# Down projection of a Strassen-type feed-forward block: product 2 in the other four PSUM banks, product 6 summed on product 1

## The chip, the cores and the metric

The kernel runs on one core of one Trainium2 chip. The metric is the device time of one execution in microseconds (us), lower is better. Each time comes from an execution on the chip; the profile is one more execution, recorded by the hardware profiler.

## The reference

The kernel computes one layer of a diffusion backbone: x is 1024 tokens by 1024 channels, all in fp32. The part that matters here is its end, with w_gate and w_up of 1024 x 2816 and w_down of 2816 x 1024:

```
def swiglu(h, w_gate, w_up, w_down):
    return (jax.nn.silu(h @ w_gate) * (h @ w_up)) @ w_down
...
x = x + g1 * mix
h2 = modulate(rmsnorm(x, norm2_g[layer]), sh2, sc2)
x = x + g2 * swiglu(h2, w_ffn_gate[layer], w_ffn_up[layer], w_ffn_down[layer])
return x
```

## The kernel before

Everything ahead of the last product, attention, projections, gate and up, is left as it is by the change. The last stage is the **down projection**, act @ w_down, and the residual x2 + g2 * (...) behind it.

The down projection is one level of the Strassen-Winograd scheme: both operands are cut into 2 x 2 blocks, and seven products of half size take the place of eight. The kernel calls them by the numbers 1, 2, 6, 7, 5, 4, 3 and runs them in this order. The seven left factors were summed before, in the feed-forward stage, and lie in DRAM (s_d). The right factors are made on the way from rows of w_down, kept in SBUF (wr, rows, lower), by `weights(n, g)`: for product 6 that is three DVE subtractions a step, of which the second writes a page t with two buffers.

A product has 11 steps g (256 rows of the inner dimension, as two halves), and each step has four output tiles i of 128 x 512. `step(n, g)` loads one page ar of the left factor by SP into the tag st (three buffers in all), makes it into a high and a low part (page a: ACT casts, DVE subtracts), and does the same with the right factor (page wd: ACT casts, POOL subtracts). Pages a and wd come from a pool yp of eight buffers, so four steps are in flight. `go` then issues three matmuls for each i: high x high, high x low, low x high. That is 12 matmuls a step, 132 a product, 924 in all.

`multiply(n, ps, first, done)` runs the 11 steps of a product on four PSUM banks ps, and calls done(i) behind the last step of tile i. `first` says whether the banks are begun anew or summed on. `banks()` takes four of the eight banks; the third call gets those of the first, the fourth those of the second. So before the change X and Z are the same four banks, and Y and W are the other four.

The outputs are put together so, with P1 to P7 for the products: u2 = P1 + P6; u3 = u2 + P7; the quarters of the output are P1 + P2 (emit(0,0)), u3 + P5 (emit(1,1)), u2 + Z, where P4 was summed on P7 (emit(1,0)), and u2 + W, where P3 was summed on P5 (written out by p3). P2 was summed on X, the banks that held P1, after ACT had copied P1 to u2; P6 went to Y and DVE added it to u2. `emit` multiplies a tile by the gate g2b, adds the residual x2t, and stores it.

The order in which each engine issues its instructions in this stage is not written by hand: a planner of the framework places them by its own forecast of when each is ready, with earlier program lines preferred, and buffers are given out by it too.

Of the kernel before, what the change touches and what calls it, by code (L numbers as in the profile page):

```python
# [13 lines left out]
ALU = mybir.AluOpType  # L14
# [74 lines left out]
def hybrid_block_kernel(  # L89
# [55 lines left out]
    PE, DVE, ACT, SP = Ordered(nc.tensor), Ordered(nc.vector), Ordered(nc.scalar), Ordered(nc.sync)  # L145
# [36 lines left out]
    def page(name, dt=F32, cols=512, tag="st"):  # L182
        return stg.tile([P, cols], dt, tag=tag, name=name)
# [74 lines left out]
    with ExitStack() as sa:  # L258
# [262 lines left out]
        for ji, (job, c0) in enumerate(jobs):  # L521
# [23 lines left out]
            for t in range(NT if job == "q" else NT + NTC):  # L545
# [29 lines left out]
                elif half:  # L575
                    st = jp.tile([P, 256], F32, tag="st", name="stc")
                    ACT.copy(st, ps[:, 256:])
                    SP.dma_start(gkc_d[(t - NT) * P:(t - NT + 1) * P, :], st)
                else:
# [10 lines left out]
                    st = jp.tile([P, 8, 64], F32, tag="st", name="str")  # L590
# [644 lines left out]
    with ExitStack() as so:  # L1235
# [62 lines left out]
        for t in range(NT - 1):  # L1298
# [3 lines left out]
            if t in E1:  # L1302
                i = len(early1)
# [70 lines left out]
    def banks3():  # L1374
        return (fps.tile([P, 512], F32, tag=n, name="f" + n) for n in "YZW")

    ops0, X, u2 = first[0]
    Y, Z, W = banks3()
# [143 lines left out]
    with ExitStack() as sf:  # L1522
# [30 lines left out]
        def step(n, g):  # L1553
            if n == 1 and g < NEARLY:
                weights(n, g)
                return early[g]
            ar = page("ar")
            r0 = (NG * (n - 1) + g) * P
            SP.dma_start(ar, s_d[r0:r0 + P, :])
            return down_pages(ar, weights(n, g), POOL)  # L1560

        def go(ps, g, a, w, i, first, last):
            s = slice(i * P, (i + 1) * P)
            st, en = first and g == 0, last and g == NG - 1
            PE.matmul(ps[i], a[:, 0, s], w[:, 0], start=st, stop=False, skip_group_check=True)
            PE.matmul(ps[i], a[:, 0, s], w[:, 1], start=False, stop=False, skip_group_check=True)
            PE.matmul(ps[i], a[:, 1, s], w[:, 0], start=False, stop=en, skip_group_check=True)

        def banks():
            return [dps.tile([P, 512], F32, tag="d", name="psdn") for _ in range(4)]  # L1570

        def multiply(n, ps, first, done, ntail=1, mid=None):
            for g in range(NG - ntail):
                if mid and g == MID:
                    mid()
                aw = step(n, g)
                for i in range(4):
                    go(ps, g, *aw, i, first, True)
            aws = [(g, *step(n, g)) for g in range(NG - ntail, NG)]
            for i in range(4):  # L1580
                for aw in aws:
                    go(ps, *aw, i, first, True)
                done(i)

        u2, u3, resid = [], [], {}
        def at(hf, c, i):
            return slice(hf * 512 + i * P, hf * 512 + (i + 1) * P), slice(c * 512, (c + 1) * 512)

        def load_x2(hf, c):
            for i in range(4):  # L1590
                t = fp.tile([P, 512], F32, tag="x2", name="x2t", bufs=NX2)
                SP.dma_start(t, x2_d[at(hf, c, i)])
                resid[hf, c, i] = t

        def emit(hf, c, i, v):
            ot = page("ot", tag="sb")
            DVE.tensor_tensor(ot, v, g2b[:, c * 512:(c + 1) * 512], op=ALU.mult)
            x2t = resid[hf, c, i]
            DVE.tensor_tensor(x2t, x2t, ot, op=ALU.add)
            SP.dma_start(out[at(hf, c, i)], x2t)  # L1600

        def p1(i):
            u2.append(fp.tile([P, 512], F32, name=f"u2{i}"))
            ACT.copy(u2[i], X[i])

        def p6(i):
            DVE.tensor_tensor(u2[i], u2[i], Y[i], op=ALU.add)

        def p7(i):
            u3.append(fp.tile([P, 512], F32, name=f"u3{i}"))  # L1610
# [17 lines left out]
        X = banks()  # L1628
# [1 line left out]
        g2b = fp.tile([P, D], F32, name="g2b")  # L1630
        SP.dma_start(g2b, mod_d[3:4, :].broadcast_to([P, D]))
        load_x2(0, 0)
        multiply(2, X, False, lambda i: emit(0, 0, i, X[i]))
        Y = banks()
        multiply(6, Y, True, p6)
        Z = banks()
        multiply(7, Z, True, p7)
        load_x2(1, 1)
# [91 lines left out]
```

## Time and profile before

| | us |
|---|---|
| runs before: median (lowest, highest) of 3 | 1598.3 (1594.61, 1601.04) |
| the profiled execution, its own time | 1597.48 |
| its span, from first to last instruction | 1595.7 |
| down projection, first to last matmul's start | 1374.9 to 1590.9 |

The profile names engines PE (TensorE matmuls), PEld (its weight loads), DVE, ACT, POOL and SP, which issues the DMAs. A row gives what an engine did, output first; an idle time in brackets is what the engine waited just before, with the instruction that ended the wait. Matmuls overlap, so the start-to-start spacing of a run of matmuls says more than the duration of one. Where the trace names tiles it leaves buffer numbers out: psdn is any of the eight banks X, Y, Z, W; u is u2 or u3.

### The profile page before, as it was taken

The page shows a single profiled execution, that of the slowest core. Times are in us where ns is not written, and L with a number is a line of the kernel's source. Part 1 is how long each engine was busy: PE and PEld are TensorE (multiplying, and loading weights), DVE is VectorE, ACT ScalarE, POOL GpSimd, SP SyncE. Part 2 cuts the span into 40 slices and gives each one's busy share as a digit, 9 for nine tenths or more (in the row PEclk, how much of TensorE's full clock was granted, in tenths as well). Part 3 has the DMA queues.
Part 4 walks back from the last instruction along what each step waited for, and adds up shares of the span by engine and source line. Part 5 has one row for each costly group of instructions (what it writes and reads, how often), then busy time and mean ns, then how long its engine had stood idle before and what let it go on. Part 6 is the DMA issues. An engine that isn't in the chain of part 4 may idle for free.

```text
span 1595.7 us, 21599 instructions
## 1 busy us (share of the span) xinstructions
PE 1531.8 (96%) x7884; PEld 1252.6 (79%) x7884; DVE 1018.4 (64%) x1598; ACT 636.1 (40%) x1221; POOL 518.1 (32%) x340
## 2 busy tenths in 40 slices
PE   6999999999999999999999999799999999999998
PEld 3678888878778887778878887688887888877886
DVE  4755469038877755553684678866666665878356
ACT  3433255158767752133212334233333333344432
POOL 3323000022211211210221422555555555256454
PEclk9999999999999999999999999999999999999999
DMA  9456666354333236416652333433333334774342
GB/s 339 128 186 215 230 220 228 107 154 125 103 114 108 87 94 218 157 58 216 225 171 67 125 120 102 150 117 100 99 100 99 99 102 129 266 255 146 99 145 99
DMA packets 171667, 235.49 MB, mean 148 GB/s; under 512 B 15580, under 2 KB 105628, under 8 KB 171560
## 3 DMA queue, kind: packets, MB, share of 16 engines
q1 hardware_dynamic: 171560, 234.11, 45.5%
q8 instruction: 62, 1.02, 0.3%
q14 instruction: 45, 0.37, 0.1%
HBM read 167.83 MB, written 66.24 MB: 147 GB/s over the span
## 4 chain that ended last, share of the span: by engine, by line
PE 76%; DVE 11%; issue 4%; DMA 4%; ACT 3%; POOL 2%; SPq 0%; DVEq 0%; ACTq 0%; POOLq 0%
PE psj L137 15%; PE psdn L137 10%; PE psd L137 9%; PE fZ L137 7%; PE fW L137 7%; PE fX L137 6%; PE pso L137 5%; PE psb L137 4%; PE fY L137 4%; PE pv L137 2%; PE pt L137 1%; ACT pb L137 1%; DVE phl L137 1%; DVE S L137 1%; DVE oT L137 1%
## 5 line engine op out<-in xcount | busy, mean ns | idle before, releaser
L137 PE MATMUL psdn<-wd,a 128*128 128x512 f32 x924 | 211.9, 390 | 4.4 <-ACT u L137 1.8
L137 PEld LDWEIGHTS psdn<-wd,a 128*128 128x128 f32 x924 | 172.7, 188 | 43.5 <-DVE a L137 3.7
L211 POOL TENSOR_TENSOR w_P<-sc,w_P 128x512 fp32r<-128x512 f32 x80 | 119.4, 1495 | 128.8 <-ACT w_P L137 125.5
L137 PE MATMUL fZ<-T,w_P 128*128 128x512 f32 x528 | 129.1, 394 | 10.3 <-DVE u L137 10.3
L211 POOL TENSOR_TENSOR w_lo<-raw,w_hi 128x1024 fp32r<-128x1024 f32 x24 | 57.6, 2400 | 235.6 <-ACT w_hi L137 218.1
L137 PE MATMUL psd<-hh,w_hi 128*128 128x512 f32 x320 | 133.4, 417 | 0.0
L137 PE MATMUL psd<-hh,w_lo 128*128 128x512 f32 x320 | 128.5, 402 | 0.0
L137 PE MATMUL psd<-hl,w_hi 128*128 128x512 f32 x320 | 127.7, 399 | 0.0
L137 PE MATMUL psj<-w_hi,hh 128*128 128x512 f32 x320 | 125.4, 393 | 0.8 <-ACT hh L137 0.8
L137 PEld LDWEIGHTS fZ<-T,w_P 128*128 128x128 f32 x528 | 100.6, 191 | 32.3 <-issue 8.9
L137 PE MATMUL psj<-w_lo,hh 128*128 128x512 f32 x320 | 125.3, 392 | 0.6 <-POOL w_lo L211 0.6
L137 PE MATMUL psj<-w_hi,hl 128*128 128x512 f32 x320 | 124.7, 393 | 0.5 <-DVE r L137 0.4
L211 POOL TENSOR_TENSOR w_P<-raw,w_P 128x512 fp32r<-128x512 f32 x56 | 87.7, 1566 | 78.0 <-ACT w_P L137 68.6
L137 ACT CAST w_P<-sc 128x512 fp32r<-128x512 f32 x88 | 54.0, 621 | 130.1 <-PE fZ L137 66.3
L137 PE MATMUL fX<-B,w_P 128*128 128x512 f32 x432 | 103.8, 389 | 0.0
L137 DVE TENSOR_TENSOR a<-ar,a 128x512 fp32r<-128x512 f32 x77 | 64.9, 855 | 58.6 <-ACT a L137 58.5
L249 POOL TENSOR_TENSOR r<-r,nhalf 128x8 f32<-128x8 f32 (+1 forms) x40 | 51.3, 1286 | 150.2 <-DVE r L137 150.2
L137 PEld LDWEIGHTS fX<-B,w_P 128*128 128x128 f32 x432 | 81.1, 188 | 16.8
L137 ACT CAST a<-ar 128x512 fp32r<-128x512 f32 x77 | 47.9, 623 | 113.9 <-PE psdn L137 64.4
L137 ACT CAST w_hi<-raw 128x1024 fp32r<-128x1024 f32 x56 | 58.1, 1049 | 53.2 <-DMA raw<-in_w_in_dram 20.3
L137 DVE SCALAR_TENSOR_TENSOR t1f<-t1f,u 128x512 f32<-128x512 f32 x66 | 61.7, 935 | 20.1 <-ACT t1f L137 19.0
L137 PEld LDWEIGHTS psj<-w_hi,hl 128*128 128x128 f32 x320 | 60.3, 189 | 14.9 <-DVE hl L137 2.4
(267 smaller groups left out, 3474.2 us busy)
## 6 DMA issues: line engine op xcount, KB each, us to landing
wm<-in_w_mod_dram SPq DMA_DIRECT2D x48, 512.0 KB
raw<-in_w_in_dram SPq DMA_DIRECT2D x40, 512.0 KB
ar<-s_d SPq DMA_DIRECT2D x77, 256.0 KB
raw<-in_w_gate_dram SPq DMA_DIRECT2D x22, 512.0 KB
raw<-in_w_up_dram SPq DMA_DIRECT2D x22, 512.0 KB
s_d<-t1f SPq DMA_DIRECT2D x44, 256.0 KB
s_d<-sa SPq DMA_DIRECT2D x33, 256.0 KB
xt<-in_x_dram SPq DMA_DIRECT2D x16, 512.0 KB
```

What stands on the lines that cost most here:

```text
L137: r = op(*args, **kw)
L211: return (lo_eng or DVE).tensor_tensor(lo, src, hi.bitcast(F32), op=ALU.subtract)
L249: POOL.tensor_tensor(r, r, nhalf[:, 0:w], op=ALU.pow)
```

## The change

Product 2 no longer sums on X but begins anew in Y, and p2 adds it to u2 (which still holds P1) in a new page v, from which emit goes on. Product 6 sums on X, which still holds P1, so X then holds P1 + P6, and ACT copies it to u2. So the four DVE additions of p6 become four ACT copies, and four DVE additions of p2 are new. The copies of P1 by p1 stay. Z still takes X's banks and W those of Y.

```
+        def p2(i):
+
+            v = page("v", tag="st")
+            DVE.tensor_tensor(v, u2[i], Y[i], op=ALU.add)
+            emit(0, 0, i, v)
+
         def p6(i):
-            DVE.tensor_tensor(u2[i], u2[i], Y[i], op=ALU.add)
+            ACT.copy(u2[i], X[i])
...
         load_x2(0, 0)
-        multiply(2, X, False, lambda i: emit(0, 0, i, X[i]))
         Y = banks()
-        multiply(6, Y, True, p6)
+        multiply(2, Y, True, p2)
+        multiply(6, X, False, p6)
         Z = banks()
         multiply(7, Z, True, p7)
```

## Rows read from the trace of the kernel before

**Rows 1.** The page's engine table: busy time, share of the span, instructions.

```profile
PE 1531.8 (96%) x7884; PEld 1252.6 (79%) x7884; DVE 1018.4 (64%) x1598; ACT 636.1 (40%) x1221; POOL 518.1 (32%) x340
```

**Rows 2.** Timeline of PE, down projection: start, length, what, count, idle before.

```profile
1374.89 30.14 PE L137 MATMUL psdn<-wd,a 128*128 128x512 f32 x132
1406.78 41.56 PE L137 MATMUL psdn<-wd,a 128*128 128x512 f32 x181 [1.75 <-ACT u L137]
1448.78 88.11 PE L137 MATMUL psdn<-wd,a 128*128 128x512 f32 x385 [0.45 <-POOL wd L211]
1537.66 30.21 PE L137 MATMUL psdn<-wd,a 128*128 128x512 f32 x132 [0.77 <-DVE a L137]
...
```

**Rows 3.** Timeline of ACT, products 1 to 6.

```profile
1406.14 2.04 ACT L137 COPY u<-psdn 128x512 f32<-128x512 f32 x4
...
1437.31 0.62 ACT L137 CAST a<-ar 128x512 fp32r<-128x512 f32 x1 [1.62 <-issue]
...
1444.61 0.62 ACT L137 CAST wd<-t 128x512 fp32r<-128x512 f32 x1 [3.96 <-DVE t L137]
```

**Rows 4.** Timelines of DVE and of PE's weight loads, products 2 and 6.

```profile
1404.67 1.76 DVE L137 TENSOR_TENSOR a<-ar,a 128x512 fp32r<-128x512 f32 x1
...
1412.17 0.68 DVE L137 TENSOR_TENSOR a<-ar,a 128x512 fp32r<-128x512 f32 x1
...
1412.90 35.00 PEld L137 LDWEIGHTS psdn<-wd,a 128*128 128x128 f32 x155 [0.34 <-DVE a L137]
...
1463.16 73.31 PEld L137 LDWEIGHTS psdn<-wd,a 128*128 128x128 f32 x324 [0.44 <-DVE a L137]
```

**Rows 5.** Timeline of DVE, end of product 2.

```profile
1437.89 1.28 DVE L137 TENSOR_TENSOR ot<-psdn,g2b 128x512 f32<-128x512 f32 x2
...
1442.09 1.28 DVE L137 TENSOR_TENSOR x2t<-x2t,ot 128x512 f32<-128x512 f32 x2
1443.29 0.68 DVE L137 TENSOR_TENSOR a<-ar,a 128x512 fp32r<-128x512 f32 x1
1443.89 0.68 DVE L137 TENSOR_TENSOR t<-lower,rows 128x512 f32<-128x512 f32 x1
```

**Rows 6.** Timeline of POOL, start of product 6.

```profile
1445.30 4.67 POOL L211 TENSOR_TENSOR wd<-t,wd 128x512 fp32r<-128x512 f32 x2 [5.49 <-ACT wd L137]
```

**Rows 7.** Chain that ended last, in order of time: start, length, what.

```profile
1402.43 2.57 DMA ar<-s_d
...
1445.30 3.43 POOL wd L211
```

**Rows 8.** Busy time by stretch: PE, PEld, DVE, ACT, POOL, clock, DMA.

```profile
1448.80:1468.00 19.20, 19.19 (x82) 15.30 (x83) 18.20 (x17) 8.04 (x15) 12.51 (x8) 1.00 0.39 118
```

**Rows 9.** Tile psdn: additions on DVE, minimum, median, maximum ns.

```profile
L137 DVE TENSOR_TENSOR u<-u,psdn x16: 674/678/682, 1468.7 to 1563.1; 128x512 f32<-128x512 f32 x16
```

**Rows 10.** Timeline of DVE after product 5: first instructions of the block, and those behind.

```profile
1526.86 1.28 DVE L137 TENSOR_TENSOR u<-u,psdn 128x512 f32<-128x512 f32 x2
...
1536.92 1.89 DVE L137 TENSOR_TENSOR a<-ar,a 128x512 fp32r<-128x512 f32 x3
```

**Rows 11.** DVE's groups from 1400 on: busy us, mean ns, idle before.

```profile
L137 DVE TENSOR_TENSOR x2t<-x2t,ot 128x512 f32<-128x512 f32 x12 | 12.7, 1097 | 0.0
...
L137 DVE TENSOR_TENSOR ot<-u,g2b 128x512 f32<-128x512 f32 x8 | 6.4, 845 | 0.0
...
L137 DVE TENSOR_TENSOR ot<-psdn,g2b 128x512 f32<-128x512 f32 x8 | 5.3, 684 | 4.9 <-PE psdn L137 4.9
```

**Rows 12.** Timeline of ACT, end of product 6.

```profile
1467.97 0.61 ACT L137 CAST wd<-wr 128x512 fp32r<-128x512 f32 x1
```

**Rows 13.** Timeline of SP, from product 2 on.

```profile
1416.75 0.91 SPq L137 DMA_DIRECT2D x2t<-x_d  x2
...
1421.96 16.35 SPq L137 DMA_DIRECT2D ar<-s_d  x8
1440.39 3.33 SPq L137 DMA_DIRECT2D out_dram<-x2t  x4
```

## The prediction, made before the change was run

> **What bounds the kernel now.** I read the page's engine table first: PE is busy for 96% of the span [rows 1]. So a change pays only by shortening PE's idle time. Next I read PE's timeline over the down projection, which shows where that idle time is: 924 matmuls in six pieces, with a gap of 1.75 us before the second, one of 0.45 before the third, and three more of 0.69 to 0.77 of which one is shown [rows 2]; 4.4 us in all. The change touches the first two, and the place between products 6 and 7, where there is no gap now.
>
> To know which instruction belongs to which step I count. The first piece, 132 matmuls, is product 1, 11 steps of 12. The piece from 1406.78 has 181 matmuls in 41.56 us, 229.6 ns each, so product 2 ends at 1406.78 + 132 x 0.2296 = 1437.1, and 49 matmuls belong to product 6: four whole steps (6,0) to (6,3) and one matmul of (6,4), written as (product, step). The piece from 1448.78 begins inside (6,4), and product 6 ends after 83 more at 88.11/385 = 228.9 ns, at 1467.8. The pool yp holds 8 pages, two a step, so ACT can cast step s only when PE has done step s - 4. The cast at 1437.31 starts as product 2 ends [rows 3], so it is (6,3), and the other steps are counted from it.
>
> **Gap one, product 1 to 2.** ACT's view shows why PE waits: the four copies of X to u2 start only at 1406.14, after casts of product 2's pages [rows 3], 1.1 us after product 1's last matmul, and PE resumes at 1406.78. The change gives product 2 the other banks, so this wait goes. What is late next is DVE. The low half of a for (2,0) runs from 1404.67 to 1406.43, and that of (2,2) starts at 1412.17 and is done at 1412.85; PE's weight loads already stop for 0.34 us until 1412.90 on that page [rows 4]. A matmul with a's low half is the third of a step, so without the copies PE could do two matmuls of (2,0) at 1405, go on from 1406.47, be about 0.7 us ahead, and then wait for (2,2) until 1412.90 all the same. DVE has no pause between those two rows, and the change takes nothing off it there. So the 1.75 us turn into a wait for DVE. I take 0; the bounds are 0 and -1.75.
>
> **Gap two, product 2 to 6.** This is where work is added. Today emit(0,0,i) is two DVE instructions, eight for four i, in one block from 1437.89 to 1443.29, 5.4 us. Behind the block in DVE's order stand the low half of (6,3) at 1443.29 and t, the weight difference of (6,4), at 1443.89 [rows 5]. ACT's cast of that t, at 1444.61, had waited 3.96 us for it [rows 3], POOL's subtraction followed at 1445.30 after 5.49 us of idleness [rows 6], took 3.43 us [rows 7], and PE resumed at 1448.78. So the chain block, t, cast, POOL, PE already sets PE's second gap. After it DVE is busy for 18.20 of 19.20 us until the end of product 6, at the upper of TensorE's two levels of the clock, 2.4 GHz (granted 1.00) [rows 8], and PE's weight loads stop for DVE's a twice more, the second time for 0.44 us [rows 4]. What is put into the block goes through to PE, since DVE has no slack behind it.
>
> The change adds four additions v = u2 + Y. Such an addition, with one operand in PSUM, takes 678 ns [rows 9]; back to back, two instructions of DVE start 1.20 us before what follows [rows 5], 0.60 each. Four are 2.4 us. That is the lower price. The upper one is the row of the same block elsewhere: after product 5, where emit also reads a page in SBUF, twelve instructions run from 1526.86 to 1536.92, 10.1 us [rows 10], which is 4.7 more than 5.4. The surplus is in instructions with both operands in SBUF, some of them beside POOL's work: x2t has a mean of 1097 ns and ot<-u of 845, while ot<-psdn has 684 [rows 11]. Below, the bound is 0: the order of issue is made by a planner, and it could put a(6,3) and t(6,4) between the additions. I take 2.4, because POOL's pause covers most of the block [rows 6]. The low half of (6,3) would then be there at about 1446.4, where PE wants it at 1437.1 + 3 x 2.755 + 2 x 0.23 = 1445.8, and w of (6,4) 2.4 us later than now.
>
> The Trainium skill, page "SBUF — State Buffer", section "Who interferes with whom", says that a DVE instruction with at most one SBUF input does not contend with GpSimd, while one with two SBUF inputs contends with a GpSimd instruction that reads SBUF, and the second to start is blocked. The trace agrees: 16 additions that read PSUM stay between 674 and 682 ns [rows 9], while those with two SBUF inputs have the higher means [rows 11]. By that rule the four ot, which now take v from SBUF, lose their immunity, and the block would cost the 4.7 us of the block after product 5 and not 2.4. It is rival two.
>
> **Product 6 to 7.** The four DVE additions at the end of product 6 are removed, and ACT copies take their place. On DVE they stood at the end of the product, and PE's next gap comes only at 1537.66 [rows 2], so their going saves nothing. The copies are new work on X, and Z takes X's banks, so product 7's first matmul now waits for the first copy, as product 2's did. ACT's last cast before that place starts at 1467.97 and ends at 1468.58 [rows 12]. Behind it the first copy, some 0.5 us (four take 2.04, rows 3), ends at 1469.1, and PE would come at 1467.8: 1.3 us. If the copies come ahead of that cast, the price is 0; if gap one repeats itself, 1.75. I take 0.9. Queued behind the copies is the cast of a step that PE needs four steps later.
>
> **The pages v.** They are taken from the tag st, whose three buffers carry ar. Now SP issues eight ar loads in one run from 1421.96, so those of (6,3) to (6,5) are in before the four stores of emit, which go out from 1440.39 on [rows 13]. With v in one of the buffers, a load of about (6,5) slips behind the stores, which then end near 1447. A load took 2.57 us from issue to landing [rows 7], a cast takes 0.61 [rows 12] and a subtraction 0.68 [rows 5]: ready at 1451, where PE wants (6,5) at 1437.1 + 5 x 2.755 + 2.4 = 1453.3. Hidden by the four steps of pages ahead; I cost it at 0.
>
> **Sum.** 0 + 2.4 + 0 + 0.9 = +3.3 us. The profiled execution took 1597.48 us and would take 1600.8; the median shown is 0.8 higher, so I give 1598.3 + 3.3 = 1601.6. A measurement of this kernel can't tell less than about 0.5%, 8.0 us, from no change.
>
> **The rivals.**
> One: the wait goes and the block is covered, because the planner puts product 6's pages between the additions. For it: DVE's order is not the program's (two ot stand together before their x2t, rows 5). Against it: emit's instructions stand closed as one block after product 2 and after product 5. It gives -1.75, 1596.6.
> Two: the block becomes as long as after product 5, from the contention told above: 4.7 + 0.9 = +5.6, 1603.9. For it: same shape, same neighbours [rows 10]. Against it: POOL's pause.
> Three, the other side: v starves ar. If the three buffers are handed out in program order, ar of (6,0) waits until v of i = 1 has been read, and stands on SP behind the four stores. Then product 6 starts only after the block (5.4 + 2.4 = 7.8), a load, a cast and a subtraction (2.57 + 0.61 + 0.68 = 3.9): 11.7 us, some 1610. It decides once ar of (6,0) is issued more than some 4 us after product 2's end. Against it: two loads of x2t at 1416.75, which the program has after product 7, were issued in the middle of product 2 [rows 13], so buffers are filled when they come free.
>
> **Chances.** Forecast 0.60 (own range 1598.5 to 1604); rival one 0.17; rival two 0.14; rival three 0.07; anything else that reorders the stage for the better 0.02. Rival three is slower by over 0.5%, and 0.01 of rival two for a pile of smaller losses: 0.08. Faster by over 0.5% would need 8 us where PE's five gaps are 4.4: 0.02. Within: 0.90. The range goes from rival one less a quarter of the spread of the three runs shown (6.4 us, so 1.6), 1595, to rival two with the copies at their upper price, 1598.3 + 4.7 + 1.75 plus the same, 1606.4, rounded up to 1607. Rival three stays outside.
>
> **What would show it.** Right: no gap of PE on ACT's u between products 1 and 2, but weight loads that wait for DVE's a until about 1412.9; a DVE block of twelve instructions from about 1437.9, some 7.8 us long; PE's gap in (6,3) and (6,4) near 3 us in place of 0.45, ended by POOL wd or DVE a; a gap of about 1 us on ACT u before product 7; the last five products otherwise as before. Wrong: product 2 ending 1.5 us earlier, DVE's block split by a and t, or PE waiting for ar at the start of product 6.

## The result, and the profile after

The changed kernel took 1608.01 us (median of seven, 1605.15 to 1613.8) against 1598.3 (1594.61 to 1601.04): a ratio of 1.006, with a 95% interval of 1.0046 to 1.0074, which is 7.4 to 11.8 us more. The forecast was 1601.6 with a range to 1607, so the time lies above the range, at the place of rival three.

The stage is measured from here on by one number, from the first to the last start of a matmul into psdn. Before it is 216.0 us (1374.9 to 1590.9), in the changed kernel 225.0 (1382.2 to 1607.2). The profiled execution of the changed kernel took 1613.8 us, the highest of its seven, because it also came to the stage 7.3 us late. Up to there the two programs issue the same instructions in the same order. The other profiles below begin the stage between 1371.9 and 1376.35, except the changed kernel's own repeat, at 1378.9. A kernel below that is the same up to there (stores on ACT) begins it at 1375.1, so I take the lateness for scatter between executions; its cause stays open. Lengths of the stage leave it out.

The page's engine table, which answers to [rows 1]: the counts are the same but for four more instructions on ACT.

```profile
PE 1543.5 (96%) x7884; PEld 1261.8 (78%) x7884; DVE 1024.0 (64%) x1598; ACT 638.5 (40%) x1225; POOL 517.1 (32%) x340
```

The timeline of PE, which answers to [rows 2]:

```profile
1382.19 30.54 PE L137 MATMUL psdn<-wd,a 128*128 128x512 f32 x134
1413.38 5.92 PE L137 MATMUL psdn<-wd,a 128*128 128x512 f32 x24 [0.66 <-DVE a L137]
1419.79 24.32 PE L137 MATMUL psdn<-wd,a 128*128 128x512 f32 x106 [0.49 <-DVE a L137]
1450.49 0.79 PE L137 MATMUL psdn<-wd,a 128*128 128x512 f32 x1 [6.38 <-ACT wd L137]
1451.85 101.37 PE L137 MATMUL psdn<-wd,a 128*128 128x512 f32 x433 [0.56 <-POOL wd L211]
1553.98 30.26 PE L137 MATMUL psdn<-wd,a 128*128 128x512 f32 x132 [0.76 <-DVE a L137]
```

The first three pieces have 134 + 24 + 106 = 264 matmuls, which is products 1 and 2 (132 each). The two end at 1444.11, 61.9 us after the start, where the forecast's counting gave 62.2 for before. Of product 6 not one matmul has been done by then. Before, 49 of them had gone through without a pause behind product 2; now PE stands for 6.38 us at the very first. The gap names ACT's cast of wd, so ACT comes next, in its own order:

```profile
1434.52 0.61 ACT L137 CAST wd<-wr 128x512 fp32r<-128x512 f32 x1
1449.30 0.62 ACT L137 CAST a<-ar 128x512 fp32r<-128x512 f32 x1 [14.17 <-DMA ar<-s_d]
1449.83 0.61 ACT L137 CAST wd<-t 128x512 fp32r<-128x512 f32 x1
```

The cast of wd only stands behind the cast of a, and that one had waited 14.17 us for a transfer of ar. SP's timeline, which answers to [rows 13], shows why:

```profile
1429.50 2.01 SPq L137 DMA_DIRECT2D ar<-s_d  x2
1445.31 0.94 SPq L137 DMA_DIRECT2D out_dram<-x2t  x2
1446.35 2.28 SPq L137 DMA_DIRECT2D ar<-s_d  x3
1448.91 0.94 SPq L137 DMA_DIRECT2D out_dram<-x2t  x2
```

In [rows 13] eight loads of ar stand ahead of the stores. Here SP issues two at 1429.50, the last that product 2 needs, and then none until 1446.35. DVE's timeline tells what happened to the three buffers in the meantime:

```profile
1434.64 0.86 DVE L137 TENSOR_TENSOR a<-ar,a 128x512 fp32r<-128x512 f32 x1 [0.86 <-ACT a L137]
1442.11 1.37 DVE L137 TENSOR_TENSOR v<-u,psdn 128x512 f32<-128x512 f32 x2 [6.61 <-PE psdn L137]
1443.39 1.29 DVE L137 TENSOR_TENSOR ot<-v,g2b 128x512 f32<-128x512 f32 x2
1444.60 1.29 DVE L137 TENSOR_TENSOR x2t<-x2t,ot 128x512 f32<-128x512 f32 x2
...
1448.20 1.29 DVE L137 TENSOR_TENSOR x2t<-x2t,ot 128x512 f32<-128x512 f32 x2
1449.95 0.69 DVE L137 TENSOR_TENSOR a<-ar,a 128x512 fp32r<-128x512 f32 x1 [0.47 <-ACT a L137]
```

The last ar of product 2 has been read at 1435.50. From then on all three buffers of the tag st lie empty, but SP loads nothing into them: they are v's, and the first v can be written only at 1442.11, when its bank of product 2 is done. The load of (6,0) goes out once the first two v have been multiplied (1443.39 to 1444.68) and the two stores ahead of it are issued. The block itself runs from 1442.11 to 1449.5, 7.4 us.

The windows (busy time of PE, PEld, DVE, ACT and POOL, then TensorE's granted clock, share and rate of DMA) show that the gap is not all:

```profile
1444.00:1446.00 2.00, 0.11 (x1) 0.00 (x0) 2.00 (x5) 0.00 (x0) 0.00 (x0) 1.00 0.00 0
1448.00:1450.40 2.40, 0.00 (x0) 0.00 (x0) 1.93 (x4) 1.10 (x2) 0.00 (x0) 0.50 0.79 273
1452.00:1454.00 2.00, 2.00 (x5) 1.62 (x6) 2.00 (x3) 0.28 (x1) 1.48 (x1) 0.50 0.54 183
1458.00:1460.00 2.00, 2.00 (x10) 1.64 (x9) 2.00 (x3) 0.61 (x2) 2.00 (x2) 0.98 0.65 233
```

The DMA engines are idle until 1446. While PE stands, the granted clock goes from 2.4 GHz (1.00) to 1.2 GHz (0.50), and it is still there when PE is busy again: 5 matmuls in the window from 1452, 10 in the one from 1458. DVE has hardly a pause in any of these windows either, but it is not what sets the pace: from 1452.44 to 1457.99 the starts of PE's matmuls lie an even 0.43 us apart, with no wait between them, and from 1458.27 on 0.23. The 13 matmuls at the lower clock cost 13 x 0.20 = 2.6 us.

### The profile page after: what moved, and what is told of

Same layout as the page of the kernel before. It is cut to its first block, busy times and chain, and to the rows that moved or that the text cites. A ratio compares the mean times of both kernels' runs of the same rounds, so it can differ in the third digit from the quotient of the medians.

```text
span 1612.0 us, 21608 instructions
## 1 busy us (share of the span) xinstructions
PE 1543.5 (96%) x7884; PEld 1261.8 (78%) x7884; DVE 1024.0 (64%) x1598; ACT 638.5 (40%) x1225; POOL 517.1 (32%) x340
## 4 chain that ended last, share of the span: by engine, by line
PE 68%; DVE 14%; issue 6%; DMA 5%; ACT 4%; POOL 2%; SPq 1%; DVEq 0%; ACTq 0%; POOLq 0%
PE psdn L137 9%; PE psd L137 9%; PE psj L137 8%; PE fZ L137 7%; PE fW L137 7%; PE fX L137 6%; PE pso L137 5%; PE psb L137 4%; PE fY L137 4%; DMA wm<-in_w_mod_dram 2%; PE pv L137 2%; PE pt L137 1%; DMA raw<-in_w_in_dram 1%; SPq L137 1%; ACT pb L137 1%
## 5 line engine op out<-in xcount | busy, mean ns | idle before, releaser
L137 DVE TENSOR_TENSOR a<-ar,a 128x512 fp32r<-128x512 f32 x77 | 69.2, 909 | 60.7 <-ACT a L137 60.6
L137 PEld LDWEIGHTS psj<-w_hi,hh 128*128 128x128 f32 x320 | 61.6, 193 | 15.2 <-ACT hh L137 2.4
```

The costliest lines, as they stand in the source:

```text
L137: r = op(*args, **kw)
```

## The experiments

The expectations speak of two theories. By the buffers theory, the loss comes from the buffers that v takes from ar, which are handed out in program order. By the block theory, it comes from the four additions themselves, in the DVE block. Each ratio is to the kernel before; the repeats ran once, without a ratio.

The stage can be cut in three by the starts of its matmuls, 132 a product: up to the last matmul of product 2, from there to the first of product 7, and the rest. The rest takes 122.6 to 122.7 us in every profile. The first part varies from 61.5 to 63.4 us whichever the kernel, but for the one that does additions in it (u2's half early, 66.2). What the change does is therefore best read from the middle part, product 6:

| kernel | stage, us | its middle part, us | median, us | ratio (95%) |
|---|---|---|---|---|
| before | 216.0 | 31.4 | 1598.3 | 1 |
| before, again | 216.8 | 31.5 | one run, 1598.63 | |
| changed | 225.0 | 40.9 | 1608.01 | 1.006 (1.0046 to 1.0074) |
| changed, again | 224.4 | 40.0 | one run, 1609.95 | |
| own buffers for v | 220.9 | 34.9 | 1599.9 | 1.0002 (0.9982 to 1.0022) |
| sum in place, no v | 220.9 | 34.9 | 1599.18 | 1.0007 (0.9992 to 1.0022) |
| in place, again | 219.4 | 34.9 | one run, 1600.96 | |
| pages v alone | 223.0 | 37.9 | 1602.51 | 1.0016 (1.0002 to 1.0031) |
| no additions | 216.4 | 31.5 | 1596.7 | 0.9993 (0.9979 to 1.0006) |
| stores on ACT | 224.8 | 40.5 | 1606.42 | 1.0037 (1.0015 to 1.0059) |
| two pages of st | 224.4 | 39.1 | 1603.85 | 1.0043 (1.002 to 1.0066) |
| u2's half early | 220.3 | 31.6 | 1600.05 | 1.0014 (1.0001 to 1.0027) |
| u2's half late | 218.8 | 33.7 | 1600.64 | 1.0024 (1.0005 to 1.0043) |

**Own buffers for v.** Against the changed kernel:

```
-            v = page("v", tag="st")
+            v = fp.tile([P, 512], F32, tag="v", name="v", bufs=4)
```

> The changed kernel with one thing altered: v comes from a tag of its own with four pages, so it no longer takes a buffer of ar. Buffers theory (v holds the three buffers of ar, loads for product 6 start only behind the block): PE's 6.4 us gap at the start of product 6 and the half clock behind it go, and the stage from the first to the last matmul of the down projection falls from 225 us to 216 to 219, the time to 1598 to 1601. Block theory (the four added DVE instructions delay product 6): all or most of the 9 us stay, stage 222 to 225, time 1605 to 1608, since the block is as long as before.

The same additions and the same block, with the ring st left to ar. The stage is 220.9, between what the two theories gave, and the time is that of before within the interval. SP issues loads of ar again ahead of product 2's end (1439.8), and PE's long gap is gone; the timelines of SP and PE:

```profile
1431.12 10.57 SPq L137 DMA_DIRECT2D ar<-s_d  x4
...
1449.21 2.79 PE L137 MATMUL psdn<-wd,a 128*128 128x512 f32 x11 [0.63 <-DVE a L137]
1453.95 89.18 PE L137 MATMUL psdn<-wd,a 128*128 128x512 f32 x385 [1.94 <-POOL wd L211]
```

Two gaps of 0.63 and 1.94 us stand where the changed kernel has 6.38 and 0.56, and they come later, inside (6,3) and (6,4).

**Sum in place.** No page at all:

```
-            v = page("v", tag="st")
-            DVE.tensor_tensor(v, u2[i], Y[i], op=ALU.add)
-            emit(0, 0, i, v)
+            DVE.tensor_tensor(u2[i], u2[i], Y[i], op=ALU.add)
+            emit(0, 0, i, u2[i])
```

> The changed kernel without a page v at all: p2 adds Y into u2 in place (product 6's copy overwrites u2 later) and emit reads u2. Buffers theory: as with pages of its own, stage 216 to 219, time 1598 to 1601. Block theory: twelve instructions in the block as ever, 1605 to 1608. What lies over the 216 us of before is then the price of the four additions, for which I had 2.4 us.

It gives 220.9 and, run again, 219.4; the middle part is 34.9 in both, as with buffers of its own. The block and what follows it, from DVE's timeline, and PE's gaps behind it:

```profile
1438.84 1.27 DVE L137 TENSOR_TENSOR u<-u,psdn 128x512 f32<-128x512 f32 x2
...
1446.65 0.68 DVE L137 TENSOR_TENSOR a<-ar,a 128x512 fp32r<-128x512 f32 x1
```

```profile
1406.82 39.97 PE L137 MATMUL psdn<-wd,a 128*128 128x512 f32 x168 [1.73 <-DVE a L137]
...
1447.39 2.81 PE L137 MATMUL psdn<-wd,a 128*128 128x512 f32 x11 [0.60 <-DVE a L137]
1452.12 89.16 PE L137 MATMUL psdn<-wd,a 128*128 128x512 f32 x385 [1.92 <-POOL wd L211]
```

The block takes 1446.65 - 1438.84 = 7.8 us, as forecast, and (6,3)'s low half follows it. The gaps are 0.60 and 1.92 us in place of 0.45. The first line is gap one: still 1.73 us, but it waits for DVE's a, as forecast. In this profile the granted clock fell behind it (last section), which cost 1.4 us and is nearly all that the repeat is shorter by.

**The pages alone.** The kernel before, with its order of products, and v only as a copy that ACT makes; no addition on DVE is added:

```
+        def p2(i):
+            v = page("v", tag="st")
+            ACT.copy(v, X[i])
+            emit(0, 0, i, v)
-        multiply(2, X, False, lambda i: emit(0, 0, i, X[i]))
+        multiply(2, X, False, p2)
```

> The kernel before, banks and products as they were, with one thing added: ACT copies X to a page v of the tag st at the end of product 2 and emit reads v. DVE's block keeps eight instructions. Buffers theory: the gap comes back without any exchange of banks, PE idle for 5 to 8 us at the start of product 6, clock at half after it, stage 222 to 226, time 1604 to 1609. Block theory: no more than 2 us over before, 1598 to 1600.

The gap comes back without the additions and without the exchange of banks; the timelines of ACT and PE:

```profile
1440.76 0.62 ACT L137 CAST a<-ar 128x512 fp32r<-128x512 f32 x1 [2.16 <-DMA ar<-s_d]
...
1441.95 0.50 PE L137 MATMUL psdn<-wd,a 128*128 128x512 f32 x1 [3.98 <-ACT wd L137]
1443.36 100.77 PE L137 MATMUL psdn<-wd,a 128*128 128x512 f32 x433 [0.91 <-POOL wd L211]
```

It is 3.98 + 0.91 us, less than in the changed kernel, whose block is longer. ACT's new copies do not make it: ACT stood idle for 2.16 us behind them until ar had landed. The stage is 6.6 us longer than the mean of before's two profiles; by the timed ratio the price is 2.6 us (0.3 to 5.0), and 1602.51 lies below the 1604 to 1609 that the buffers theory gave. That the pages cost by themselves is shown, how much is not.

**No additions.** The changed kernel without P1 in one quarter of the output, which leaves out that part of the sum:

```
-            v = page("v", tag="st")
-            DVE.tensor_tensor(v, u2[i], Y[i], op=ALU.add)
-            emit(0, 0, i, v)
+            emit(0, 0, i, Y[i])
```

> The changed kernel with the four additions v = u2 + Y and the page v left out: emit reads Y directly, so one quarter of the output lacks P1. DVE's block is back to eight instructions, the exchange of banks and ACT's copies of product 6 stay. If the additions are the whole rest that the version in place has over before (stage 220.9 against 216.0 us), the stage falls to 215 to 217.5 us and the time to 1597 to 1600, and PE's gaps in (6,3) and (6,4) are 0.5 us or less in sum, with no stretch at a lower clock. If the exchange itself costs something (the copies of product 6 ahead of product 7), 1 to 2 us stay.

The exchange of banks and the copies between products 6 and 7 alone: 216.4, the mean of before's two profiles. They neither cost nor bring anything. PE's gap behind the block is 0.44 us again, and the granted clock stays at 1.00:

```profile
1446.18 88.13 PE L137 MATMUL psdn<-wd,a 128*128 128x512 f32 x385 [0.44 <-POOL wd L211]
```

**The stores on ACT.** If SP's order is what holds the loads up, the changed kernel gains when the four stores of p2 leave SP. emit gets a parameter for the queue:

```
-            emit(0, 0, i, v)
+            emit(0, 0, i, v, ACT)
```

> The changed kernel with emit's four stores after product 2 issued by ACT and not by SP. It asks how much of the gap is SP's order (the loads of ar stand behind the first two stores) and how much the buffers. Buffers theory: ar of product 6 can go when v of i = 1 has been read, some 1.6 us sooner than now, so PE's gap falls from 6.4 to about 4.8 us and the time by 1.5 to 2.5, to 1605 to 1607; ACT's casts could stand behind the stores' waits and take it back. If SP's order alone made the gap, most of the 6.4 goes: 1599 to 1601.

SP issues the first load of ar at 1437.77, 0.64 us after product 2's end (1437.13) and as soon as ot of i = 1 has read its v (1436.41 + 1.29 = 1437.70). In the changed kernel it was 2.24 us, so 1.6 us of that delay was the stores. But it brings next to nothing, 224.8. The timelines of SP and ACT show where it went:

```profile
1437.77 3.88 SPq L137 DMA_DIRECT2D ar<-s_d  x3
...
1440.35 0.62 ACT L137 CAST a<-ar 128x512 fp32r<-128x512 f32 x1 [12.47 <-DMA ar<-s_d]
...
1441.94 0.94 ACTq L137 DMA_DIRECT2D out_dram<-x2t  x2
1442.92 0.62 ACT L137 CAST wd<-t 128x512 fp32r<-128x512 f32 x1 [1.96 <-DVE x2t L137]
```

The cast of wd now stands on ACT behind the second pair of stores, which wait for DVE's x2t. PE's gap is 6.46 us.

**Two pages of st.** v of i = 0 and 1 as in the changed kernel, the other two in place:

```
-            v = page("v", tag="st")
+            v = page("v", tag="st") if i < 2 else u2[i]
```

> The changed kernel with v from the tag st for i = 0 and 1 alone; for i = 2 and 3 the sum is made in place in u2. Buffers theory, three buffers handed out in the order of the program: ar of (6,0) gets the buffer of ar (2,10) and is loaded in good time, ar of (6,1) and (6,2) wait for the two pages v. PE starts product 6 without a gap and stops at (6,1), some 3 to 5 us in place of 6.4 and later by one step, stage 220 to 224, time 1602 to 1606. If buffers went to whoever needs one first, ar would be loaded during product 2 as with pages of its own: stage 221 or less and no wait for ar at all.

By program order one buffer is left for (6,0), and (6,1) must wait. It does; the timelines of ACT and PE:

```profile
1429.38 0.62 ACT L137 CAST a<-ar 128x512 fp32r<-128x512 f32 x1 [3.13 <-DMA ar<-s_d]
...
1438.75 0.62 ACT L137 CAST a<-ar 128x512 fp32r<-128x512 f32 x1 [8.22 <-DMA ar<-s_d]
...
1441.99 1.68 PE L137 MATMUL psdn<-wd,a 128*128 128x512 f32 x5 [4.22 <-DVE a L137]
```

The two casts are those of (6,0) and (6,1). So the order in which the buffers are handed out is shown. The time is another matter: 224.4, as long as with four pages, where the theory gave 220 to 224. PE did eight matmuls of (6,0) and stopped for 4.22 us, since the subtraction of (6,0)'s page stands in DVE's order behind the block, though DVE was idle for 7.22 us ahead of the block. Why the planner put it there stays open.

**u2's half of the sum ahead of product 2's end.** If the additions cost because they stand in the block, their work on u2 can go earlier: u2*g2 is added to x2t during product 2, and the block is back to eight instructions. Eight more stand elsewhere. In the first of two kernels the planner places them, in the second they are held back until the last page of product 2 has been subtracted, into DVE's pause before the block. The first kernel's edit, in part:

```
-            v = page("v", tag="st")
-            DVE.tensor_tensor(v, u2[i], Y[i], op=ALU.add)
-            emit(0, 0, i, v)
+            emit(0, 0, i, Y[i])
+        def early2():
+            for i in range(4):
+                ot = page("ot", tag="sb")
+                DVE.tensor_tensor(ot, u2[i], g2b[:, 0:512], op=ALU.mult)
+                x2t = resid[0, 0, i]
+                DVE.tensor_tensor(x2t, x2t, ot, op=ALU.add)
...
+        multiply(2, Y, True, p2, 1, early2)
```

> The changed kernel with the sum taken apart: in the middle of product 2 DVE adds g2 x P1 to the residual (eight instructions, u2 is ready then), and at the end of product 2 emit takes Y alone from PSUM, so the block at the end has eight instructions, no page v. Buffers and block theories together: the gap at the start of product 6 goes and the additions are off the chain; stage 214.5 to 217.5, time 1596 to 1600, level with before or better by up to 1.5 us. If DVE has no room in product 2 either, product 2's pages come late and the stage is 218 or more.

> The version with the sum taken apart once more, but g2 x P1 is added to the residual only behind the subtraction of product 2's last page a (an order edge on DVE), where the trace of before has DVE idle for about 6 us between 1425 and 1436. Theory: an added DVE instruction costs PE time only where DVE itself ends PE's wait; in that place eight of them, 4.8 us, fit in, so the stage is 216 to 217.5 us (the version without the additions has 216.4, the one with them in the middle of product 2 220.3), the time 1596 to 1599. Rival: DVE is the bound of this stage as a whole, so the eight instructions cost the same wherever they stand: stage 219 or more, 1600 or more.

The planner put the eight at 1414 to 1422, amid product 2's pages, and PE got three waits for DVE there, 2.05 us in sum:

```profile
1418.25 3.04 PE L137 MATMUL psdn<-wd,a 128*128 128x512 f32 x12 [1.07 <-DVE a L137]
1421.75 3.01 PE L137 MATMUL psdn<-wd,a 128*128 128x512 f32 x12 [0.47 <-DVE a L137]
1425.27 27.49 PE L137 MATMUL psdn<-wd,a 128*128 128x512 f32 x119 [0.51 <-DVE a L137]
```

Held back, they found DVE free but POOL at work:

```profile
1430.33 2.37 DVE L137 TENSOR_TENSOR ot<-u,g2b 128x512 f32<-128x512 f32 x2
...
1432.62 1.28 DVE L137 TENSOR_TENSOR x2t<-x2t,ot 128x512 f32<-128x512 f32 x2
1433.83 3.48 DVE L137 TENSOR_TENSOR ot<-u,g2b 128x512 f32<-128x512 f32 x2
```

The eight took 8.1 us (1430.33 to 1438.43), not 8 x 0.6 = 4.8. The Trainium skill, page "SBUF — State Buffer", section "Who interferes with whom", says that a DVE instruction with two SBUF inputs contends with a GpSimd (POOL) instruction that reads SBUF, and that the order of issue decides which of the two is blocked. The trace agrees here: POOL worked from 1430.13 to 1431.55 and from 1433.40 to 1436.76, the two pairs that began just behind its starts took 2.37 and 3.48 us, and the pair between them, begun while POOL was idle, took 1.28.

The stage is 218.8, 2.4 longer than without the additions: less than in the block by the profiles (219.4 to 220.9), not by the timed ratios, and near the 219 of the rival. What is less is not the waiting: PE stands for 1.97 + 0.57 us here and for 0.60 + 1.92 in place, which is 2.1 us over the 0.45 of before in both; in the early half it is 2.05 + 0.54, again 2.1 over. In place the granted clock falls behind the gaps, here and in the early half it stays up (last section). So the idle time that the added work brings was the same in all three places, as the rival has it. No version that computes the whole output is faster than the kernel before.

**Repeats.** Before, changed and in place once more, side by side on another chip:

> The kernel before once more, for the repeatability of the stage in a profile: 215.5 to 217 us from the first to the last matmul of the down projection (216.0 in the first profile), with the gap on ACT's copies of u at 1.5 to 2 us. If it moves by more than 1 us, differences of the experiments below 1 us say nothing.

> The changed kernel once more: stage 224 to 226 us (225.0 in its first profile), PE's gap at the start of product 6 of 6.2 to 6.6 us and about 10 us at the lower clock. The 7 us that its first profile lost ahead of the stage should not come back if they were chance.

> The version in place once more: stage 219.5 to 221.5 us (220.9 before). The part up to the end of product 2, which took 63.4 us there and 61.9 in the changed kernel, moves with the landing of w_down's rows and may differ by 1 us.

216.8, 224.4 and 219.4: the lengths repeat within 0.8 us, in place within 1.5; the middle parts within 0.9 in the changed kernel and 0.1 in the other two. In the repeat of the changed kernel PE waits for 6.59 us at the same place:

```profile
1447.69 0.80 PE L137 MATMUL psdn<-wd,a 128*128 128x512 f32 x1 [6.59 <-ACT wd L137]
```

## Why the prediction was wrong

The middle part takes the loss apart. It is 31.4 and 31.5 us before, 31.5 without the additions, 34.9 in all three profiles that have the additions in the block and no page of st, and 40.9 and 40.0 in the changed kernel. So the exchange of banks is worth 0, the additions cost 3.4 to 3.5 and the pages v 5.1 to 6.0; together 8.6 to 9.4, inside the timed 7.4 to 11.8. The timed ratios divide it otherwise: changed to in place is 1.006/1.0007 = 1.0053, 8.5 us, which leaves little for the additions. With the halves of the two intervals put together as a root of squares, 0.0014 and 0.0015 giving 0.0021, that is 5.1 to 11.8 us, and in place to before is 1.1 us (-1.3 to 3.5). Both agree that the pages are the larger part; how much larger isn't settled.

**The pages v: the step that failed.** "Hidden by the four steps of pages ahead; I cost it at 0." The cover did not exist. It was worked out for one load slipping behind the stores, about (6,5), as if a buffer went to whichever page could use it first. A buffer of a tag goes to the pages in program order, and four v stand in the program between the last ar of product 2 and ar of (6,0). So all of the look-ahead was lost, from (6,0) on, and the term taken at 0 measured 5.1 to 6.0 us. Own buffers and the sum in place, which take v out of the ring and leave the additions in the block, bring the middle part to 34.9; the pages alone, without any addition, bring the long gap back; with two pages the load of (6,1) is held back and that of (6,0) is not.

**Rival three had the mechanism, with a chance of 0.07.** What spoke against it, the two loads of x2t at 1416.75 that went out ahead of their turn in the program [rows 13], was read wrongly. They fill buffers of another tag, and show only that tags don't wait for one another. The point that was to decide it, ar of (6,0) issued 4 us after product 2's end, was too late: 2.24 us did it (1446.35 - 1444.11), since everything from the load to PE came behind. Its price of 11.7 us put the load behind all four stores, and so added the whole block to it. In fact the load of (6,0) waits only until v of i = 1 has been read, as the kernel with the stores on ACT shows plainly, and then for two stores; PE stood for 6.38 + 0.56 = 6.9 us, 6.5 over before. On top came 2.6 us of the lower clock, which the rival did not have: 9.1 of the 9.4 that the middle part grew by. So its 1610 came near the median by luck, from a sum that was put together wrongly.

**Gap two: the right mechanism, 2.4 us taken, 3.4 to 3.5 measured.** The block grew by four additions to 7.8 us in place and 7.4 in the changed kernel, and without pages of st PE waited in (6,3) and (6,4), first for DVE's a and then for POOL's wd, all as forecast. By the timed ratio of in place to no additions, 1.0007/0.9993 = 1.0014, it is 2.2 us, with an interval of -1.0 to 5.5. Of the 3.4 to 3.5 in the profiles, 2.1 is idle time of PE, near the forecast. The rest was not foreseen: the two short gaps bring the clock down as well, for 1.4 to 1.6 us (below).

**Rival two, the contention in the block, did not happen.** POOL was idle through the block. Its timeline, and the tile v in the changed kernel, minimum, median and maximum in ns:

```profile
1450.52 2.96 POOL L211 TENSOR_TENSOR wd<-t,wd 128x512 fp32r<-128x512 f32 x2 [13.87 <-ACT wd L137]
...
L137 DVE TENSOR_TENSOR ot<-v,g2b x4: 683/684/687, 1443.4 to 1447.6; 128x512 f32<-128x512 f32 x4
```

The four ot that take v from SBUF are as fast as those that read psdn [rows 11], which is the choice that the forecast made because of POOL's pause. The contention came in the kernel with the late half, where POOL had work.

**Gap one: right.** The wait for ACT's copies turned into waits for DVE's a, 0.66 + 0.49 us in the changed kernel and 1.73 in place. The first part of the stage is 62.0 and 62.7 us before and 61.5 to 63.4 with the exchange of banks, so nothing is seen of a gain.

**The copies between products 6 and 7: 0.9 taken, 0 measured.** One piece of 433 matmuls runs from (6,0) through product 7 and on, and the middle part without additions is that of before. ACT's timeline in the changed kernel:

```profile
1483.87 2.04 ACT L137 COPY u<-psdn 128x512 f32<-128x512 f32 x4
```

The forecast let the first copy stand behind a cast that ends after product 6. Here ACT's casts were through in time: the first of the four ends at 1484.44, and product 7's first matmul starts at 1484.60 without a wait.

**Rival one: refuted.** Even without the additions the stage is 216.4 and the first part no shorter, so there was no 1.75 us to win.

## What to carry to other kernels

A page that is written at the end of one phase must not come from the ring that prefetches the next: the ring hands its buffers out in program order, so pages that come late hold empty buffers, and the load that they hold back is the one that the next phase needs first. Before a page's tag is taken for free, count who else uses it and what stands next in line for its buffers. And where an engine sets another's gap, as DVE does here, look for a place for added work where its own queue is free and no other engine gets in its way; neither of the two earlier places tried here was such a place.

## What the runs showed of the hardware that was not expected

A gap of PE can cost more than its length. In the changed kernel the granted clock fell to 0.50 in the gap of 6.38 us and was back at 0.98 only in the window from 1458; PE's matmuls started 0.43 us apart in place of 0.23 until then, 2.6 us in sum (1.4 in the repeat). It fell even where no gap was longer than 2 us; windows of the sum in place:

```profile
1449.00:1452.00 3.00, 1.20 (x6) 0.64 (x4) 1.95 (x4) 1.35 (x3) 3.00 (x1) 1.00 0.91 265
1452.00:1455.00 3.00, 2.88 (x7) 2.30 (x8) 2.90 (x4) 1.11 (x2) 1.72 (x3) 0.55 0.48 171
1455.00:1458.00 3.00, 3.00 (x13) 2.40 (x13) 3.00 (x5) 1.18 (x3) 1.72 (x2) 0.88 0.23 87
```

Gaps of 0.60 and 1.92 us stand before and in the first of them, with PE busy for 1.20 of 3 us; the next window has a mean of 0.55 and 7 matmuls, the third 13. In the three profiles of own buffers and in place this cost 1.4 to 1.6 us. The kernel before, with one gap of 0.45 us there, shows 1.00 in the stretch behind it [rows 8].

The length of a gap does not decide it. Here are the stretches behind gap one of the sum in place (1.73 us) and of the kernel before, again (2.40 us), and the one with the gap of 1.97 us in the late half:

```profile
1408.00:1411.00 3.00, 3.00 (x8) 2.32 (x8) 3.00 (x6) 1.44 (x3) 0.41 (x1) 0.50 0.94 348
...
1407.70:1411.00 3.30, 3.27 (x14) 2.74 (x15) 3.30 (x4) 2.16 (x5) 1.02 (x1) 1.00 0.65 241
...
1445.00:1450.00 5.00, 3.03 (x14) 2.52 (x14) 5.00 (x10) 0.90 (x2) 0.62 (x2) 1.00 0.76 263
```

Behind the shortest of the three gaps the clock fell, behind the others it did not. What decides it is not shown here, and so the price of a gap of this size can't be told in advance from these runs.
